# The recurrent block of a hybrid decoder trunk: one written-out order on all engines, the softplus at another place, the first transfers in another order

## Chip, cores and metric

The kernel runs on one core of a Trainium2 chip. The metric is the device time of one execution in microseconds (us), as the median of the runs. Beside it stands one profiled execution, whose trace gives the start, the duration and the releaser of instructions on each engine: TensorE (PE in the rows; PEld is its weight load), VectorE (DVE), ScalarE (ACT), GpSimd (POOL), and SyncE (SP), which issues the DMAs.

## Reference

Two layers over a sequence of 1024 positions and 1024 channels: a recurrent block (RG-LRU) with a feed-forward network, then stick-breaking attention with a feed-forward network; RMS norms lie ahead of each part. The change touches the recurrent block of the first layer:

```python
def rg_lru_block(x, w_in, b_in, conv_w, conv_b, gate_w, gate_b, lam, w_out, b_out):
    u = jnp.einsum("bsd,de->bse", x, w_in) + b_in
    gate_branch, rec = u[..., :LRU_WIDTH], u[..., LRU_WIDTH:]
    rec = causal_depthwise_conv(rec, conv_w, conv_b)             # 4 taps
    rec_blk = rec.reshape(bsz, seq, N_LRU_BLOCKS, LRU_BLOCK)     # 4 blocks of 256
    gl = jnp.einsum("bsnc,gncd->gbsnd", rec_blk, gate_w).reshape(2, bsz, seq, LRU_WIDTH)
    r_gate, i_gate = jax.nn.sigmoid(gl[0] + gate_b[0]), jax.nn.sigmoid(gl[1] + gate_b[1])
    log_a = -LRU_C * r_gate * jax.nn.softplus(-lam)
    a = jnp.exp(log_a)
    b = jnp.sqrt(-jnp.expm1(2.0 * log_a)) * (i_gate * rec)
    _, h = lax.associative_scan(_linear_recurrence_combine, (a, b), axis=1)
    y = jax.nn.gelu(gate_branch, approximate=True) * h
    return jnp.einsum("bse,ed->bsd", y, w_out) + b_out
```

## The kernel before

**Layout and products.** Everything is kept transposed, with channels on the 128 partitions and positions along the row, in halves of 512 positions (`NB`; n = 0, 1). A product of fp32 numbers is made of three matmuls in a rounded fp32 type (fp32r): high by high (L128), high weight by low data (L129), low weight by high data (L130). So each weight of 128x1024 is loaded into a raw tile by SyncE, cast on ScalarE (`whi`, L115), and its low half (`wlo`, L119) is a subtraction on VectorE. Data are split likewise: `xh`, `xl` for the normed input and later for the block's output, `rh`, `rl` for the recurrent columns. Weights stand in a ring of six tiles, that is three weights; raw tiles are three.

**Start (L249–L323).** The input and the weights of the first four columns (`FIRST`) are loaded in eight slices. As each slice k arrives, ScalarE casts (`fh`, `xh`) and squares it, VectorE makes the low halves and adds the squares into `sacc`, and TensorE adds the slice's matmuls for the four columns, first half. Then the sum of squares over channels is made by TensorE with a column of ones (`column_stats`, L192–L197, in the rows `a_ps<-ones,sacc`). VectorE works out the row factors 1/rms (`ms`, `rs_s`, `rs_t`, `rcol`, L161–L170), TensorE spreads them over the partitions (`spread`, L172, in the rows `a_ps<-ident,rcol`), and VectorE copies them from PSUM into `rbc0` and `rbc1` (L312). Both row factors borrow one bank, `bank`, which is the second half of the fourth column; the matmuls of the second halves (`second`) stand between them. Here the order on all engines is that of the code (`manual_schedule`, L249).

**Softplus (L332–L366).** Some 40 operations of VectorE on 128x8 values give the decay constants `cc` and `ch` from lambda, and the bias of the convolution `cb` and `nbias`, by a row of operations of which each needs the one before. They stand behind the start in the code, where a scheduler places every engine's instructions but TensorE's; it has put them between the rows of the start.

**The block (L326–L475).** For eight column tiles e of 128 channels there are four kinds of steps, in the order of a written string (L473): A e projects recurrent column e and makes the four convolution taps (L397–L409: VectorE's `u` halves by `rbc` L401, ScalarE's first tap, three taps on VectorE L405, then `rh` and `rl` L408); B e projects gate column e (`gb`, L447) and takes its GELU; G b makes the gates of columns 2b and 2b+1 from both (`g_ps`), and for each the values `ga`, `gt`, `gs` (L429–L439) and the scan into `y` (L440); Y e multiplies `y` by the GELU (L452). `ptile` (L383) hands out PSUM: `psA` and `psB` (`psl[0]`, `psl[1]`) hold two tiles of two banks each, and fill all eight banks; the pools take turns, two tiles each. TensorE runs in the order of the string, written by hand; where instructions of the other engines stand is the scheduler's choice.

**Last column (L455–L470).** B7 is projected half by half, each into a tile of its own from `psl[1]` (L459). Behind a half, VectorE multiplies by `rbc` (L461), ScalarE takes the GELU, and the whole output of that half is split for the next product: `xh` on ScalarE (L466), `xl` on VectorE (L467). Behind the first half the first three weights of the output projection are loaded and split (`Mix`, L140–L158).

**Output projection (L670–L701).** It closes the pools of the block, opens six tiles of one bank (`ob_ps`) in their place, and goes through 16 output tiles, each with 24 matmuls over k = 0 to 7 (`dense_in`, L132), which need `xh` and `xl` of that k; VectorE then adds bias and residual (L699). From here on the change alters nothing.

Of the kernel before, what the change touches and what calls it, by code (L numbers as in the profile page):

```python
# [31 lines left out]
FIRST = (ND, ND + 1, 0, ND + 2)  # L32


@with_exitstack
def trunk(
# [95 lines left out]
    def dense_in(ps, w, n, nk=ND):  # L132
        for k in range(nk):
            mm3(ps, w[0][:, k], w[1][:, k], xh[k][n], xl[k][n], k == 0, k == nk - 1)
# [112 lines left out]

    lc = lst.enter_context(tc.tile_pool(name="lc", bufs=1))
    with ExitStack() as st, tc.manual_schedule(engines={E.PE, E.Activation, E.DVE, E.Pool, E.SP}):  # L249
# [34 lines left out]
        for i in range(8):  # L284
# [32 lines left out]
        second(0, range(4, ND))  # L317
        column_stats(sacc[1], bank, 1)
        second(1, range(4))
        spread_to(1)  # L320
        second(1, range(4, ND))
        second(2, range(ND))
        second(3, range(ND))  # L323


    with ExitStack() as st:  # L326
        lp = st.enter_context(tc.tile_pool(name="lp", bufs=1, reuse_waits="tile"))
        sm = lambda name: lc.tile([P, ND], F32, name=name)
        V = nc.vector
# [35 lines left out]
        for j in range(3):  # L365
            V.tensor_scalar_mul(nbias[:, :, j], bin_rec, -1.0)  # L366

        col = lambda base, i: vc[:, base + i : base + i + 1]
# [4 lines left out]
        def load_gate(b):  # L373
            raw = rp.tile([P, D], F32, tag="raw", name="rawg")
            nc.sync.dma_start(raw, lru_gate_w[b])
            hi, lo = split(raw)
            v4 = lambda t: t.rearrange("p (g k c) -> p g k c", g=2, k=2)
            return v4(hi), v4(lo)


# [7 lines left out]
        def project_col(j):  # L388
            w = load_cols(lru_w_in[j])
            ps = ptile("a_ps")  # L390
            for n in range(NH):
                project(ps, w, n)
            return ps


        def stage_a(e):
            ps = pa.pop(ND + e) if ND + e in pa else project_col(ND + e)  # L397
            u = lp.tile([P, S + 16], F32, tag="u", name="u", bufs=2)
            V.tensor_copy(u[:, 0:3], nbias[:, e, 0:3])
            for n in range(NH):  # L400
                V.tensor_mul(u[:, 3 + n * NB : 3 + (n + 1) * NB], half(ps, n), rbc[n])  # L401
            rc = wide("rec", 3)
            nc.scalar.activation(rc, u[:, 3 : S + 3], AF.Identity, bias=cb[:, e : e + 1], scale=col(V_CW + 3 * ND, e))
            for j in range(3):
                V.scalar_tensor_tensor(rc, u[:, j : j + S], col(V_CW + j * ND, e), rc, op0=ALU.mult, op1=ALU.add)  # L405
            rh, rl = wide("rh", 3, F32R), wide("rl", 3, F32R)
            nc.scalar.copy(rh, rc)
            V.tensor_sub(rl, rc, f32(rh))  # L408
            rec[e], rech[e], recl[e] = rc, rh, rl  # L409


        def stage_g(b):
            gh, gl = load_gate(b)
            for i in range(2):
                e = 2 * b + i
                c = slice(i * P, (i + 1) * P)
                pss = []
                for g in range(2):
                    ps = ptile("g_ps")
# [23 lines left out]
        def stage_b(e):  # L443
            ps = pa.pop(e) if e in pa else project_col(e)
            gb = wide("gb", 3)
            for n in range(NH):
                V.tensor_mul(half(gb, n), half(ps, n), rbc[n])  # L447
# [1184 lines left out]
```

## Time and profile before

| what | value |
|---|---|
| runs | median 2216.97 us (2216.7 to 2217.77, 3 runs) |
| profiled execution | 2218.56 us |
| its span, first to last instruction | 2216.8 us |
| mean granted clock of TensorE | 0.992 |
| TensorE busy | 2177.2 us (98%), 10050 matmuls |
| VectorE busy | 1721.9 us (78%) |
| ScalarE busy | 1152.7 us (52%) |
| GpSimd busy | 224.1 us (10%) |
| DMA | 273.50 MB, mean 123 GB/s |

The stretch that the change touches is about the first 250 us of the span: the first matmul of the output projection starts at 242.78 us. In a row of the timeline the first number is the start in us from the span's beginning, the second the duration; then come engine, line of the code, operation, what is written and read, and in brackets how long the engine had been idle and what ended that. Rows that group instructions give the busy time and the mean of one in ns behind a bar, and the idle time ahead of them behind a second. A row with a window gives there the span of the window, the busy time of the instructions asked for (with their number), the granted clock, the DMA share and GB/s. Rows of waits give the total, the number and the longest.

### The profile page before, as it was taken

How to read it: one execution, taken by the hardware profiler on the slowest of the kernel's cores; microseconds unless marked ns; L12 is line 12 of the kernel's file. 1: busy time of each engine (PE TensorE's matmuls, PEld its weight loads, DVE VectorE, ACT ScalarE, POOL GpSimd, SP SyncE). 2: the span in 40 equal slices, each digit the busy share in tenths (PEclk: the TensorE clock that was granted, in tenths of full speed). 3: DMA queues.
4: the chain of work that ended last, by engine and by line, in shares of the span. 5: the costliest groups of instructions: out<-in, count | busy, mean ns of one | idle time of the engine just before them, and what ended most of it. 6: DMA issues, size and time to landing. Idle time of an engine off the chain costs nothing.

```text
span 2216.8 us, 28236 instructions
## 1 busy us (share of the span) xinstructions
PE 2177.2 (98%) x10050; PEld 1805.3 (81%) x10050; DVE 1721.9 (78%) x2412; ACT 1152.7 (52%) x2033; POOL 224.1 (10%) x356
## 2 busy tenths in 40 slices
PE   9899999999999999999999999999999999999997
PEld 7788888888888888878888888878888888888886
DVE  7877778677777887868888888866876777788886
ACT  5657545344444544646666666653534444454455
POOL 0000020000000000003333333421000000000001
PEclk9999999999999999999999999989999999999998
DMA  4021312334444864453333333631133444466442
GB/s 172 10 67 48 124 38 72 105 119 157 143 155 131 278 192 122 145 143 86 88 94 97 104 86 105 186 125 61 46 106 120 152 147 146 145 237 228 126 145 86
DMA packets 132316, 273.50 MB, mean 123 GB/s; under 512 B 15312, under 2 KB 22608, under 8 KB 132176
## 3 DMA queue, kind: packets, MB, share of 16 engines
q1 hardware_dynamic: 131600, 270.86, 38.9%
q8 instruction: 79, 1.29, 0.2%
q10 hardware_dynamic: 576, 0.85, 0.1%
q14 instruction: 61, 0.50, 0.1%
HBM read 175.70 MB, written 70.78 MB: 111 GB/s over the span
## 4 chain that ended last, share of the span: by engine, by line
PE 83%; DVE 9%; ACT 4%; DMA 2%; issue 1%; SPq 1%; DVEq 0%; ACTq 0%
PE p_ps L130 18%; PE p_ps L128 18%; PE p_ps L129 18%; PE qk_ps L130 3%; PE qk_ps L128 2%; PE qk_ps L129 2%; PE ob_ps L129 2%; PE ob_ps L128 2%; PE ob_ps L130 2%; PE wt_ps L1454 2%; PE a_ps L130 2%; PE a_ps L128 2%; PE a_ps L129 2%; DVE F L1442 2%; PE z_ps L1417 1%
## 5 line engine op out<-in xcount | busy, mean ns | idle before, releaser
L1443 POOL TENSOR_TENSOR w<-w,F 128x128 f32<-128x128 f32 (+1 forms) x192 | 184.6, 962 | 314.9 <-DVE F L1440 176.1
L128 PE MATMUL p_ps<-vh,wbh 128*128 128x512 f32 x524 | 204.3, 390 | 2.0 <-ACT ta L1003 2.0
L130 PE MATMUL p_ps<-vh,wcl 128*128 128x512 f32 x524 | 204.2, 390 | 0.5 <-DVE wcl L630 0.5
L130 PE MATMUL p_ps<-vh,wbl 128*128 128x512 f32 x524 | 204.3, 390 | 0.0
L130 PE MATMUL p_ps<-vh,wal 128*128 128x512 f32 x524 | 204.1, 390 | 0.1
L128 PE MATMUL p_ps<-vh,wch 128*128 128x512 f32 x524 | 204.1, 390 | 0.0
L128 PE MATMUL p_ps<-vh,wah 128*128 128x512 f32 x524 | 203.9, 389 | 0.0
L129 PE MATMUL p_ps<-vl,wch 128*128 128x512 f32 x524 | 203.9, 389 | 0.0
L129 PE MATMUL p_ps<-vl,wbh 128*128 128x512 f32 x524 | 203.9, 389 | 0.0
L129 PE MATMUL p_ps<-vl,wah 128*128 128x512 f32 x524 | 203.9, 389 | 0.0
L616 ACT CAST wbh<-sb 128x1024 fp32r<-128x1024 f32 (+2 forms) x69 | 69.6, 1009 | 192.6 <-DVE sb L600 192.6
L1440 DVE TENSOR_TENSOR_SCAN F<-F,unit 128x128 f32<-128x128 f32 (+3 forms) x128 | 126.9, 992 | 5.4 <-ACT F L1436 5.4
L1463 ACT CAST th<-wt_ps 128x512 fp32r<-128x512 f32 x192 | 93.3, 486 | 71.8 <-PE wt_ps L1454 69.8
L1464 DVE TENSOR_TENSOR tl<-wt_ps,th 128x512 fp32r<-128x512 f32 x192 | 105.1, 548 | 28.9 <-ACT th L1463 27.8
L128 PE MATMUL qk_ps<-vh,whi 128*128 128x512 f32 x264 | 118.8, 450 | 0.6 <-ACT vh L208 0.6
L128 PEld LDWEIGHTS p_ps<-vh,wbh 128*128 128x128 f32 x524 | 98.4, 188 | 22.6 <-ACT ta L1003 2.5
L130 PEld LDWEIGHTS p_ps<-vh,wcl 128*128 128x128 f32 x524 | 98.4, 188 | 21.8 <-DVE wcl L630 1.4
L130 PEld LDWEIGHTS p_ps<-vh,wbl 128*128 128x128 f32 x524 | 98.4, 188 | 21.7 <-DVE wbl L620 1.3
L130 PEld LDWEIGHTS p_ps<-vh,wal 128*128 128x128 f32 x524 | 98.4, 188 | 21.4 <-DVE wal L611 1.0
L129 PEld LDWEIGHTS p_ps<-vl,wah 128*128 128x128 f32 x524 | 98.4, 188 | 20.3
L129 PEld LDWEIGHTS p_ps<-vl,wch 128*128 128x128 f32 x524 | 98.4, 188 | 20.3
L128 PEld LDWEIGHTS p_ps<-vh,wah 128*128 128x128 f32 x524 | 98.4, 188 | 20.3
(408 smaller groups left out, 5725.9 us busy)
## 6 DMA issues: line engine op xcount, KB each, us to landing
raw<-in_ffn_w_in SPq DMA_DIRECT2D x88, 512.0 KB, 3.8
vl<-pd SPq DMA_DIRECT2D x128, 256.0 KB, 3.7
pd<-U SPq DMA_DIRECT2D x90, 256.0 KB, 2.3
raw<-in_ffn_w_out SPq DMA_DIRECT2D x28, 512.0 KB, 4.1
raw<-in_attn_w_qkv SPq DMA_DIRECT2D x24, 512.0 KB, 3.6
acc<-pd SPq DMA_DIRECT2D x28, 256.0 KB, 2.6
pph<-rbc SPq DMA_DIRECT2D x28, 256.0 KB, 2.5
ppl<-acc SPq DMA_DIRECT2D x28, 256.0 KB, 2.6
```

Of the source, the lines that this page charges most:

```text
L128: nc.tensor.matmul(ps, lhsT=wh, rhs=mh, start=first, stop=False, **kw)
L129: nc.tensor.matmul(ps, lhsT=wh, rhs=ml, start=False, stop=False, **kw)
L130: nc.tensor.matmul(ps, lhsT=wl, rhs=mh, start=False, stop=last, **kw)
L616: nc.scalar.copy(self.full(self.wb), self.full(self.sb))
L1417: nc.tensor.matmul(ps[:, 0 : c1 - c0], lhsT=lhsT, rhs=KL[q][hx][:, c0:c1], start=False, stop=True)
L1440: nc.vector.tensor_tensor_scan(rev, rev, unit[:, NB - n :][:, ::-1], first, op0=ALU.mult, op1=ALU.add)
L1442: nc.vector.tensor_tensor_scan(rev, rev, rev, first, op0=ALU.mult, op1=ALU.bypass)
L1443: nc.gpsimd.tensor_mul(wt, wt, F[:, 1 : n + 1])
L1454: nc.tensor.transpose(tp[:, c : c + P], W[q, hx, j, kb // 4][:, (kb % 4) * P : (kb % 4 + 1) * P], ident)
L1463: nc.scalar.copy(th[:, q0:], tp[:, q0:])
L1464: nc.vector.tensor_sub(tl[:, q0:], tp[:, q0:], f32(th)[:, q0:])
```

## The change

**The block's order.** Each operation of the block becomes a task of a list planner (`Plan`), with an engine, a duration in us, the tasks it waits for, and a rank. `emit` goes through the tasks in time: of those whose predecessors are placed it takes the one that can begin first (then the lowest rank), and emits it. The block stands under `manual_schedule` for TensorE, ScalarE, VectorE and GpSimd, so that this order is that of the program on all of them. `lru_plan` writes the tasks in the order of the same string. A DMA takes 2.6 us from issue to landing in the plan, an engine's hand-over 0.15 us, a change of ScalarE's function table 1.3 us.

```diff
+class Plan:
+    def emit(self):
+        left, end, free, table = set(range(len(self.tasks))), {}, dict(self.free), {}
+        while left:
+            best = None
+            for i in left:
+                eng, us, _, after, rank, tab = self.tasks[i]
+                if any(a not in end for a in after):
+                    continue
+                begin = max([free[eng], *(end[a] + (0.0 if self.tasks[a][0] == eng else 0.15) for a in after)])
+                if tab is not None and table.get(eng) != tab:
+                    begin += 1.3
+                key = (begin, rank, i)
+                if best is None or key < best:
+                    best = key
...
+def lru_plan(plan, order, fn):
+    col, rank = 5.44, {w: i for i, w in enumerate(order)}
...
+    def weights(i):
+        w = wants[i]
+        r = rank.get(w, len(order)) - 2.5
+        ld = plan.add("dma", 2.6, fn["load", w], [lo.get(i - 3), loads.get(i - 1)], r)
+        hi = plan.add("act", 1.05, fn["hi", w], [ld, his.get(i - 1), used.get(i - 3)], r)
+        lo[i] = plan.add("dve", 1.16, fn["lo", w], [hi], r)
...
+                rh = plan.add("act", 1.05, fn["rh", e], [t, GE.get((e - 3) // 2)], r)
+                rl[e] = plan.add("dve", 1.16, fn["rl", e], [rh], r)
...
+                    need = [pe, wt, rl[e // 2 * 2], rl[e // 2 * 2 + 1], *freed[cur % 4]]
+                    pe = plan.add("pe", col / 2, fn["pg", e, g], need, s_)
...
+    for n in range(NH):
+        pe = plan.add("pe", col, fn["pe", last, n], [pe, lo[i] if i in lo else weights(i), *freed[cur % 4]], r)
+        if n == 0:
+            used[i] = pe
+        m = plan.add("dve", 0.62, fn["bm", ND - 1, n], [pe, Y.get(ND - 4), Y.get(ND - 2)], r)
...
+            c = plan.add("act", 0.58, fn["xh", d, n], [y, pe], r)
+            plan.add("dve", 0.62, fn["xl", d, n], [c], r)
...
+    for k in range(3):
+        weights(wants.index(f"out{k}"))
```

(`used[i]` is the task behind which the tiles of weight i count as free.) The operations are those of before, as small functions; two of them, and the last column's tiles, which come from `ptile` now and so take part in the turn of the two pools:

```diff
+        def pe_last(w, n):
+            PS[w, n] = ptile("a_ps")
+            project(PS[w, n], W[w], n)
...
+        def b_half(e, n):
+            if n == 0:
+                gel[e] = wide("gb", 3)
+            w = f"B{e}"
+            ps = half(PS[w], n) if e < ND - 1 else half(PS[w, n], n)
+            V.tensor_mul(half(gel[e], n), ps, rbc[n])
...
-                ps = psl[1].tile([P, S], F32, tag="b", name="a_ps")
-                project(ps, w, n)
...
-        with tc.manual_schedule(engines={E.PE}):
+        with tc.manual_schedule(engines={E.PE, E.Activation, E.DVE, E.Pool}):
+            plan = Plan(pe=27.5, dve=37.5, act=31.0, dma=20.0)
...
+            plan.emit()
```

On VectorE, at the end of the block, the new list ends its work for the last column with these rows (`xl_0` and `xl_1` are the low halves of the output's first and second 512 positions, the names y the scan results, of which y_605 is column 7's, `gb` the GELU columns, `rbc_81` and `rbc_82` the row factors of the two halves):

```order
L640 TENSOR_TENSOR xl_1_109<-y_600,xh_1_93 128x512
L640 TENSOR_TENSOR xl_1_111<-y_601,xh_1_95 128x512
L640 TENSOR_TENSOR xl_1_113<-y_602,xh_1_97 128x512
L640 TENSOR_TENSOR xl_1_115<-y_603,xh_1_99 128x512
L637 TENSOR_TENSOR y_604<-y_604,gb 128x1024
L607 TENSOR_TENSOR gb<-a_ps,rbc_81 128x512
L632 TENSOR_TENSOR gs<-gs,gt 128x1024
L633 SCALAR_TENSOR_TENSOR y_605<-ga,gs 128x1024
L640 TENSOR_TENSOR xl_0_116<-y_604,xh_0_100 128x512
L638 TENSOR_TENSOR y_605<-y_605,gb 128x512
L607 TENSOR_TENSOR gb<-a_ps,rbc_82 128x512
```

Ahead of these rows stand eight more `xl`, and ahead of them `wlo` of the third output weight. In the list of before, from the scan of the last column on (y_603 there), the same place reads:

```order
L440 SCALAR_TENSOR_TENSOR y_603<-ga,gs 128x1024
L467 TENSOR_TENSOR xl_0_112<-y_600,xh_0_96 128x512
L452 TENSOR_TENSOR y_602<-y_602,gb 128x1024
L467 TENSOR_TENSOR xl_0_114<-y_601,xh_0_98 128x512
L465 TENSOR_TENSOR y_603<-y_603,gb 128x512
L156 TENSOR_TENSOR wlo<-raw,whi 128x1024
L467 TENSOR_TENSOR xl_0_116<-y_602,xh_0_100 128x512
L467 TENSOR_TENSOR xl_0_118<-y_603,xh_0_102 128x512
L156 TENSOR_TENSOR wlo<-raw,whi 128x1024
L461 TENSOR_TENSOR gb<-a_ps,rbc_82 128x512
L467 TENSOR_TENSOR xl_1_105<-y_596,xh_1_89 128x512
L467 TENSOR_TENSOR xl_1_107<-y_597,xh_1_91 128x512
```

The copy of the second half (`gb<-a_ps,rbc_82`) stood ahead of all `xl_1` rows, behind two of the output weights' low halves. It now stands behind the third weight's low half, twelve `xl` of both halves, column 7's scan and five rows around it, and is the nineteenth row after the weight's.

On TensorE, at the same place, the list of the change goes from the last column to the output projection like this (`a_ps_1743` is the tile of the last column's second half, `ob_ps_1910` the first output tile; the words in brackets are the engines on which a row waits):

```order
L268 MATMUL a_ps_1743<-xh7_1_103,whi_1585 128x512
L269 MATMUL a_ps_1743<-xl7_1_119,whi_1585 128x512
L270 MATMUL a_ps_1743<-xh7_1_103,wlo_1586 128x512
L268 MATMUL ob_ps_1910<-xh0_0_88,whi_1669 128x512 [waits DVE_49,Activation_49]
L269 MATMUL ob_ps_1910<-xl0_0_104,whi_1669 128x512
L270 MATMUL ob_ps_1910<-xh0_0_88,wlo_1670 128x512
```

and that of before, with `a_ps_1771` and `ob_ps_1908`, like this:

```order
L128 MATMUL a_ps_1771<-xh7_1_103,whi_1704 128x512
L129 MATMUL a_ps_1771<-xl7_1_119,whi_1704 128x512
L130 MATMUL a_ps_1771<-xh7_1_103,wlo_1706 128x512
L128 MATMUL ob_ps_1908<-xh0_0_88,whi_1759 128x512 [waits Activation_49]
L129 MATMUL ob_ps_1908<-xl0_0_104,whi_1759 128x512 [waits DVE_49]
L130 MATMUL ob_ps_1908<-xh0_0_88,wlo_1760 128x512
L128 MATMUL ob_ps_1908<-xh1_0_90,whi_1759 128x512 [waits Activation_49]
L129 MATMUL ob_ps_1908<-xl1_0_106,whi_1759 128x512 [waits DVE_49]
```

No matmul moved; the first output matmul now has a wait for VectorE beside that for ScalarE. Its tile is in both programs the first bank of the block's PSUM. The tile of the second half of B7 was one of `psB` in the program of before, and is the one of `psA` that begins at that bank in the program of the change.

**The third pair of gates.** On VectorE, ahead of the gates of columns 4 and 5, whose last low half is `rl` (`u` and `gb` read halves of A5 and B3, `rec` are taps, `gs`, `gt` and y belong to the gates of columns 2 and 3), the list of the change has, behind the first `u` half of A5 and four rows on `ga` and `gt`:

```order
L600 SCALAR_TENSOR_TENSOR gt<-ga 128x1024
L541 TENSOR_TENSOR wlo<-raw,whi 128x1024
L574 TENSOR_TENSOR u<-a_ps,rbc_82 128x512
L583 SCALAR_TENSOR_TENSOR rec<-u,vc,rec 128x1024 x2
L632 TENSOR_TENSOR gs<-gs,gt 128x1024
L633 SCALAR_TENSOR_TENSOR y_600<-ga,gs 128x1024
L632 TENSOR_TENSOR gs<-gs,gt 128x1024
L633 SCALAR_TENSOR_TENSOR y_601<-ga,gs 128x1024
L583 SCALAR_TENSOR_TENSOR rec<-u,vc,rec 128x1024
L541 TENSOR_TENSOR wlo<-raw,whi 128x1024
L607 TENSOR_TENSOR gb<-a_ps,rbc_81 128x512
L623 TENSOR_TENSOR rl<-rec,rh 128x1024
```

and that of before, from the first `u` half of A5 on to the row ahead of its `rl`, with two `u` rows of A6 among them:

```order
L401 TENSOR_TENSOR u<-a_ps,rbc_81 128x512
L439 TENSOR_TENSOR gs<-gs,gt 128x1024
L401 TENSOR_TENSOR u<-a_ps,rbc_82 128x512
L440 SCALAR_TENSOR_TENSOR y_599<-ga,gs 128x1024
L452 TENSOR_TENSOR y_598<-y_598,gb 128x1024
L405 SCALAR_TENSOR_TENSOR rec<-u,vc,rec 128x1024
L119 TENSOR_TENSOR wlo<-rawg,whi 128x1024
L405 SCALAR_TENSOR_TENSOR rec<-u,vc,rec 128x1024
L401 TENSOR_TENSOR u<-a_ps,rbc_81 128x512
L405 SCALAR_TENSOR_TENSOR rec<-u,vc,rec 128x1024
L401 TENSOR_TENSOR u<-a_ps,rbc_82 128x512
L119 TENSOR_TENSOR wlo<-raw,whi 128x1024
```

The two `u` halves of A5 stood two rows apart and its taps close behind; now six rows of the gates ahead and a weight's low half stand between the two halves, two pairs of `gs` and scan between the second tap and the third, and a `gb` half of B3 ahead of `rl`.

**Softplus.** It stands in the code between the first row factors and the second statistics (new L456 to L495), under the fixed order of the start:

```diff
         spread_to(0)
-        second(0, range(4, ND))
-        column_stats(sacc[1], bank, 1)
...
+        V.scalar_tensor_tensor(az, lam, -1.0, lam, op0=ALU.mult, op1=ALU.max)
...
+            V.tensor_scalar_mul(nbias[:, :, j], bin_rec, -1.0)
+        second(0, range(4, ND))
+        column_stats(sacc[1], bank, 1)
```

On VectorE the list of before has, from the first `ms` on (`rcol` are the row factors, `kq` a value of the softplus):

```order
L196 TENSOR_SCALAR ms<-a_ps 128x4
L350 SCALAR_TENSOR_TENSOR kq<-kq,gq 128x8 x2
L166 RECIPROCAL rs_s<-rs_s 128x4
L350 SCALAR_TENSOR_TENSOR kq<-kq,gq 128x8
L167 TENSOR_TENSOR rs_t<-rs_s 128x4
L350 SCALAR_TENSOR_TENSOR kq<-kq,gq 128x8
L168 TENSOR_TENSOR rs_t<-rs_t,ms 128x4
L350 SCALAR_TENSOR_TENSOR kq<-kq,gq 128x8
L169 TENSOR_SCALAR rs_t<-rs_t 128x4
L350 SCALAR_TENSOR_TENSOR kq<-kq,gq 128x8
L170 TENSOR_TENSOR rcol<-rs_s,rs_t 128x4
L351 SCALAR_TENSOR_TENSOR pq<-kq,pq 128x8
```

and the copy of `rbc_81` and the second `ms` follow five rows later. The list of the change has, around the second `ms`:

```order
L490 TENSOR_TENSOR cb<-cb,vc 128x8
L491 TENSOR_TENSOR cb<-cb,vc 128x8
L492 TENSOR_TENSOR cb<-cb,vc 128x8
L493 TENSOR_TENSOR cb<-cb,vc 128x8
L495 TENSOR_SCALAR nbias<-vc 128x8 x3
L336 TENSOR_SCALAR ms<-a_ps 128x4
L306 RECIPROCAL rs_s<-rs_s 128x4
L307 TENSOR_TENSOR rs_t<-rs_s 128x4
L308 TENSOR_TENSOR rs_t<-rs_t,ms 128x4
L309 TENSOR_SCALAR rs_t<-rs_t 128x4
L310 TENSOR_TENSOR rcol<-rs_s,rs_t 128x4
L453 COPY rbc_82<-a_ps 128x512
```

The rows of the softplus stood ahead of the first `ms` and between the first factors' rows; all 42 now lie between the copy of `rbc_81` and the second `ms`, these being the last.

**First transfers.** ScalarE's queue took the first slice of weights and the table of vectors; now it takes the first slice of the input, and SyncE's queue takes the table, then weights and input by turns. The cast of the first slice's weights moves to VectorE, and there are ten warm-up matmuls on `bank` for eight.

```diff
-        nc.scalar.dma_start(f4(fr[0]), lru_first[0])
-        nc.scalar.dma_start(vc, table)
+        nc.scalar.dma_start(xr[0][0], x[0, 0])
+        nc.sync.dma_start(vc, table)
         for k in range(ND):
-            nc.sync.dma_start(xr[k][0], x[k, 0])
+            nc.sync.dma_start(f4(fr[k]), lru_first[k])
             if k:
-                nc.sync.dma_start(f4(fr[k]), lru_first[k])
+                nc.sync.dma_start(xr[k][0], x[k, 0])
...
-            nc.scalar.copy(fh[k], fr[k])
+            (nc.scalar.copy if k else V.tensor_copy)(fh[k], fr[k])
```

**First output tiles.** The first four tiles of the output projection are taken together: each first gets its matmuls for k = 0 to 5, then each in turn those for k = 6 and 7.

```diff
+                            if k == 0:
+                                four = [pp.tile([P, NB], F32, tag="p", name="ob_ps") for _ in dn]
+                                for t, (d_, n_) in zip(four, dn):
+                                    dense_in(t, mix.w[d_], n_, range(ND - 2))
+                            ps = four[k]
+                            dense_in(ps, mix.w[d], n, range(ND - 2, ND))
```

More of the change, by code (lines that the diff above doesn't have):

```diff
@@ L366, in trunk @@
             V.tensor_scalar_mul(nbias[:, :, j], bin_rec, -1.0)
+        second(0, range(4, ND))
+        column_stats(sacc[1], bank, 1)
+        second(1, range(4))
+        spread_to(1)
+        second(1, range(4, ND))
+        second(2, range(ND))
+        second(3, range(ND))
+    with ExitStack() as st:
+        lp = st.enter_context(tc.tile_pool(name="lp", bufs=1, reuse_waits="tile"))
         col = lambda base, i: vc[:, base + i : base + i + 1]
```

302 lines of the change are left out of this document (209 added, 93 removed).

## Prediction

> **What bounds the kernel now.** I read the page first: shares by engine, then the chain that ended last.
>
> ```profile
> span 2216.8 us, 28236 instructions
> PE 2177.2 (98%) x10050; PEld 1805.3 (81%) x10050; DVE 1721.9 (78%) x2412; ACT 1152.7 (52%) x2033; POOL 224.1 (10%) x356
> PE 83%; DVE 9%; ACT 4%; DMA 2%; issue 1%; SPq 1%; DVEq 0%; ACTq 0%
> ```
>
> TensorE is busy for 98% of the span and makes 83% of the chain. The change adds two 128-column warm-up matmuls and takes none away, so it can only act on the 39.6 us in which TensorE stands idle (2216.8 − 2177.2) and on the clock at which it runs. The second view is TensorE's waits in the stretch that the change touches (0 to 260 us):
>
> ```profile
> PE a_ps L130 <- DVE wlo L119: 5.6, 1, 5.6
> PE a_ps L129 <- DVE xl L272: 1.6, 1, 1.6
> PE a_ps L175 <- DVE rcol L170: 1.2, 1, 1.2
> PE a_ps L128 <- ACT xh L269: 1.1, 1, 1.1
> PE ob_ps L129 <- DVE xl L467: 0.2, 1, 0.2
> ```
>
> That is all there is to win: one wait of 5.6 us for the low half of a weight, about 2.7 us at the first matmuls, 1.2 us at the first row factors. The stretch after the 5.6 us wait costs more than the wait, as busy time by window shows (the column after the count is the granted clock):
>
> ```profile
> 95.00:104.00 9.00, 9.00 (x41) 1.00 0.00 0
> 104.30:109.84 5.54, 0.00 (x0) 0.90 0.00 0
> 109.84:115.60 5.76, 5.76 (x14) 0.50 0.47 136
> 115.60:125.00 9.40, 9.40 (x43) 1.00 0.23 87
> ```
>
> For 5.76 us the clock is at half. Matmuls of 512 columns then start every 0.43 us, at full clock every 0.23 us (the starts in these timeline rows):
>
> ```profile
> 1444.59 0.63 PE L129 MATMUL ob<-vl,whi 128*128 128x512 f32 x1
> 1445.02 0.63 PE L130 MATMUL ob<-vh,wlo 128*128 128x512 f32 x1
> 242.78 0.39 PE L128 MATMUL ob_ps<-xh,whi 128*128 128x512 f32 x1
> 243.01 0.39 PE L129 MATMUL ob_ps<-xl,whi 128*128 128x512 f32 x1
> ```
>
> So 5.76 us did the work of 3.1, a loss of 2.7 us. VectorE is nearly full beside TensorE here, and its list therefore decides what comes late.
>
> **The change part by part.** The sum is made against the profiled execution (2218.56 us, span 2216.8); the median of the runs is 2216.97, and the shift is carried over to it.
>
> (a) *The wait of 5.6 us goes.* Its weight in the timeline, both halves:
>
> ```profile
> 103.69 1.05 ACT L115 CAST whi<-raw 128x1024 fp32r<-128x1024 f32 x1 [2.98 <-PE a_ps L129]
> 108.57 1.22 DVE L119 TENSOR_TENSOR wlo<-raw,whi 128x1024 fp32r<-128x1024 f32 x1
> ```
>
> ScalarE's cast was done at 104.74, and VectorE made the low half only at 108.57, behind other rows. In the new lists that half stands ahead of its column with a column's time to spare, and what stands there late instead is (d). Gain 5.6 + 2.7 = 8.3 us; bounds 5.6 and 8.4.
>
> (b) *Start, softplus.* The rows of the row factors now:
>
> ```profile
> 36.40 0.16 DVE L196 TENSOR_SCALAR ms<-a_ps 128x4 f32<-128x4 f32 x1
> 37.04 0.16 DVE L167 TENSOR_TENSOR rs_t<-rs_s 128x4 f32<-128x4 f32 x1
> 37.24 0.16 DVE L168 TENSOR_TENSOR rs_t<-rs_t,ms 128x4 f32<-128x4 f32 x1
> 37.85 1.16 PE L175 MATMUL a_ps<-ident,rcol 128*128 128x128 f32 x8 [1.16 <-DVE rcol L170]
> 41.63 0.95 PE L194 MATMUL a_ps<-ones,sacc 128*128 128x1 f32 x8
> 45.31 1.05 PE L175 MATMUL a_ps<-ident,rcol 128*128 128x128 f32 x8
> ```
>
> The softplus leaves the stretch ahead of the first factors (some 30 small rows at 0.08 to 0.2 us, and one weight half of 1.1 us less), so I put them 2.4 us earlier, at 35.4. It now stands whole between the first factors and the second `ms`: some 37 rows that each need the one before, at 0.20 us a step (37.04 to 37.24), and five at 0.08, 7.8 us. With the factor matmuls and their copy (1.2 + 0.6) ahead and 1.5 us from `ms` to `rcol` behind (36.40 to 37.85), the second factors come at 35.4 + 11.1 = 46.5, against 45.31: a loss of 1.2 us, whatever the start gains. That is the answer for the new order of the first transfers and for the ten warm-up matmuls too: matmuls that begin 1.5 to 4 us sooner meet this wait. Bounds 0 and 2.5.
>
> (c) *Clock at that wait.* From 35.4 TensorE has 1.2 us of factors, 24 matmuls at 0.23 and 0.95 of statistics, 7.6 us: it is done at 43.0 and idle for 3.5 us. No wait of that length stands in this stretch. The nearest below is 2.9 us, where the clock did fall; the nearest above is the 5.6 us wait, with its 2.7 us:
>
> ```profile
> 1440.81 1.12 PE L1389 MATMUL vt_ps<-ident,t 128*128 128x128 f32 x4 [2.91 <-DVE t L1364]
> 1436.00:1440.00 4.00, 1.90 (x10) 1.00 1.05 395
> 1440.00:1453.60 13.60, 10.16 (x34) 0.50 0.56 200
> ```
>
> I take 1.5 us, between 0 and 2.7, since the matmuls resume about when the clock falls rather than after.
> The Trainium skill, in "TensorE: Matmul & The Clock Gate" (Part 1, The HAM clock gate), has the clock fall after an idle window of about 3.4 us that runs free of the kernel. By that rule 3.5 us of idle seldom hold a whole window, and the sum below would be 1.5 us less. The trace speaks against it: the clock fell behind 2.9 us of idle.
>
> (d) *Third pair of gates.* VectorE's list takes the first half of a column's tile well ahead of the second, but in the rows of before such a reader waits for the whole tile:
>
> ```profile
> DVE gb L447 <- PE a_ps L130: 15.9, 4, 5.6
> ```
>
> 5.6 us is one more half of 24 matmuls at 0.23. If that holds for A5, VectorE stands idle until both halves are done, then has in order u, six gate rows, `wlo`, u, the wait for ScalarE's tap, two taps, two pairs of `gs` and scan, a tap, `wlo`, gb and `rl`: by the durations quoted in (e) and for a tap by this row 24.8 us in all.
>
> ```profile
> L405 DVE SCALAR_TENSOR_TENSOR rec<-u,vc,rec 128x1024 f32<-128x1024 f32 x24 | 30.5, 1282 | 0.2
> ```
>
> TensorE has two columns ahead of these gates (21.8) and 0.9 us of matmuls that need only the even tile: it waits 2.1 us. Bounds 0 (the reader gets its half at once) and 5.
>
> (e) *The end of the block*, the largest term. In the row lists of the change TensorE's first `ob_ps` matmul waits for VectorE, and of before it does not. The tile of the last column's second half used to come from the second pool; now the turn of the pools gives it the first one, where `ob_ps` starts. So `ob_ps` waits for VectorE's last copy (L607). Before, that copy ran 6 us after `ob_ps` had begun (at 242.78, in a row above), and nothing waited for it:
>
> ```profile
> 249.03 0.70 DVE L461 TENSOR_TENSOR gb<-a_ps,rbc 128x512 f32<-128x512 f32 x1
> 237.00:250.00 13.00, 12.81 (x57) 1.00 0.13 41
> ```
>
> In the new list it stands behind 19 rows, the first of which, `wlo` of the third output weight, cannot start until TensorE is done with the last column: that weight takes the last column's place in a ring of three. Durations (mean ns) from the groups of 225 to 256 us:
>
> ```profile
> L155 ACT CAST whi<-raw 128x1024 fp32r<-128x1024 f32 x3 | 3.1, 1047 | 0.5 <-PE a_ps L129 0.5
> L156 DVE TENSOR_TENSOR wlo<-raw,whi 128x1024 fp32r<-128x1024 f32 x3 | 3.7, 1226 | 0.0
> L467 DVE TENSOR_TENSOR xl<-y,xh 128x512 fp32r<-128x512 f32 x16 | 10.3, 696 | 0.7 <-ACT xh L466 0.7
> L452 DVE TENSOR_TENSOR y<-y,gb 128x1024 f32<-128x1024 f32 x1 | 1.2, 1227 | 0.0
> L461 DVE TENSOR_TENSOR gb<-a_ps,rbc 128x512 f32<-128x512 f32 x2 | 1.4, 694 | 0.0
> L439 DVE TENSOR_TENSOR gs<-gs,gt 128x1024 f32<-128x1024 f32 x2 | 2.4, 1224 | 2.0 <-ACT gt L437 2.0
> L440 DVE TENSOR_TENSOR_SCAN y<-ga,gs 128x1024 f32<-128x1024 f32 x2 | 4.6, 2292 | 0.1
> L465 DVE TENSOR_TENSOR y<-y,gb 128x512 f32<-128x512 f32 x2 | 1.4, 699 | 0.0
> 249.63 4.31 DVE L467 TENSOR_TENSOR xl<-y,xh 128x512 fp32r<-128x512 f32 x7
> ```
>
> Seven `xl` take 4.31 us, 0.60 a step (VectorE starts the next row 0.09 before the last ends). From TensorE's last matmul: cast 1.05, `wlo` 1.2, twelve `xl` 7.2, y 1.1, gb 0.6, gs 1.2, scan 2.2, `xl` 0.6, y 0.6, gb 0.7, and 0.2 of hand-overs: **15.6 us** by VectorE's rows with no wait between. Three hand-overs and one slow start of an `xl` behind ScalarE add about 0.9: 16.5 us. I take ScalarE's casts and square root to end ahead of the rows that need them. Bounds 12 (the cast finds its place before the column's last matmuls, by half of the twelve `xl`, 3.6 us) and 19 (the square root is late by the 2.0 us of L439's row, and 0.5 more).
>
> (f) *Clock after it.* 16.5 us idle is three times the 5.6 us wait, so 2.7 us are lost again; bounds 1.5 and 3.4. The 0.2 us wait of before at `ob_ps` goes, since the first four output tiles now leave the last two slices for later; from there on both programs have the same rows, TensorE-bound, and nothing takes the delay back.
>
> Sum: −8.3 + 1.2 + 1.5 + 2.1 + 16.5 + 2.7 − 0.2 = **+15.5 us**, that is 2216.97 + 15.5 = 2232.
>
> **The rivals.** *TensorE is not held at the end* (the side of the gain): the first output matmul's wait for VectorE is met early, by a row ahead of the twelve `xl`. For it speaks that the wait is printed without the row that it names; against it, that bank and order agree. Then (e) and (f) fall away: 15.5 − 19.2 = −3.7, 2213, not slower. It decides from a wait of about 4 us: the other terms are a gain of 3.7, and only a longer wait makes the kernel slower. *The clock stays up over 3.5 us of idle*: (c) is zero, 2231; for it speaks the 1.2 us wait without a fall, against it the fall behind 2.9 us. *More such waits*: the list has VectorE wait at the first half of several tiles, as the 15.9 us row has it four times already; if two more reach TensorE as in (d), with a fall of the clock at one, 2232 + 2 x 2.1 + 1.5 = 2238. Against it: most columns have a whole column's slack behind them.
>
> **How the numbers follow.** Forecast 0.50, clock up 0.30, more waits 0.13, not held 0.07. Range: the bounds of (b), (c), (d) and (f) seldom fall together; (e) alone moves it by −4.5 and +2.5, and the low end also takes in (c) at zero and some of (d): 2225; the high end is the rival with more waits: 2238. A measurement of this kernel tells about 0.2% (4.4 us) from no change: 2213 is −0.17%, so of the 0.07 most is "same": 0.05, and 0.02 faster; slower 0.93.
>
> **What would show it.** In the changed kernel's waits of TensorE a row `ob_ps` L268 from DVE gb L607 with 15 to 18 us, and half clock in the window behind it; a row for `rcol` L310 with about 3.5 us in its longest; no row of 5 us for `wlo`; a wait of about 2 us at `g_ps` for `rl`. If the first row is missing or under 4 us, (e) is wrong, and with it the sign. If the second factors come before 45.3, (b) is.

## The result, and the profile after

The changed kernel takes 2230.82 us (median of 4 runs, 2227.97 to 2233.80) against 2217.37 us for the kernel before in the same set (4 runs): a ratio of 1.0060, 95% interval 1.0043 to 1.0078. It is slower by 13.5 us. The profiled execution, the slowest of the four, took 2233.80 us, with a span of 2232.0 us against 2216.8.

The page of the changed kernel shows TensorE with nearly the same busy time as before (2176.1 us; before 2177.2) in a longer span:

```profile
span 2232.0 us, 28249 instructions
PE 2176.1 (97%) x10054; PEld 1803.0 (81%) x10054; DVE 1727.5 (77%) x2413; ACT 1149.8 (52%) x2030; POOL 225.4 (10%) x356
```

The difference is idle time of TensorE. Its waits in the first 260 us (total, number, longest):

```profile
PE ob_ps L268 <- ACT xh L639: 16.6, 1, 16.6
PE a_ps L315 <- DVE rcol L310: 5.4, 2, 3.3
PE a_ps L426 <- POOL ident masks.py:199: 1.4, 1, 1.4
PE g_ps L269 <- DVE rl L623: 1.3, 1, 1.3
PE g_ps L268 <- ACT rh L589: 0.5, 1, 0.5
PE a_ps L269 <- DVE xl L413: 0.2, 1, 0.2
```

The row of 5.6 us for `wlo` is gone, `rcol` has grown from 1.2 to 5.4 us in two waits, `g_ps` has two rows that were not there, and the first `ob_ps` waits for 16.6 us. A lower clock stands behind three of these places, as the busy time by window shows (the column after the count is the granted clock):

```profile
44.00:48.00 4.00, 2.57 (x13) 0.86 0.00 0
48.00:52.00 4.00, 4.00 (x14) 0.72 0.24 65
160.00:164.00 4.00, 2.24 (x8) 0.86 0.40 121
164.00:168.00 4.00, 4.00 (x14) 0.71 0.03 10
256.00:260.00 4.00, 3.30 (x8) 0.50 0.99 340
260.00:264.00 4.00, 4.00 (x16) 0.76 0.84 321
```

Where the time went is read best from the starts of the same matmuls in the timelines of the two profiled executions (`e8_all` is an experiment below):

| first matmul of | before | change | difference | e8_all |
|---|---|---|---|---|
| first row factors (`rcol`) | 37.85 | 34.53 | −3.3 | 32.58 |
| second row factors | 45.31 | 45.43 | +0.1 | 41.27 |
| first pair of gates | 71.03 | 72.81 | +1.8 | 67.00 |
| second pair of gates | 123.11 | 116.33 | −6.8 | 110.52 |
| column behind the third pair | 177.50 | 174.63 | −2.9 | 164.91 |
| output projection (`ob_ps`) | 242.78 | 256.70 | +13.9 | 230.19 |
| feed-forward (`p_ps`) | 330.31 | 346.27 | +16.0 | 317.23 |
| end of the span | 2216.8 | 2232.0 | +15.2 | 2202.0 |

The change was 6.8 us ahead at the second gates. It lost 3.9 us at the third pair, 16.8 at the end of the block and 2.0 behind it.

The long wait is best seen from VectorE's timeline, as the prediction had listed its rows:

```profile
240.96 1.23 DVE L541 TENSOR_TENSOR wlo<-raw,whi 128x1024 fp32r<-128x1024 f32 x1 [1.08 <-ACT whi L537]
242.10 7.48 DVE L640 TENSOR_TENSOR xl<-y,xh 128x512 fp32r<-128x512 f32 x12
249.49 1.22 DVE L637 TENSOR_TENSOR y<-y,gb 128x1024 f32<-128x1024 f32 x1
250.63 0.68 DVE L607 TENSOR_TENSOR gb<-a_ps,rbc 128x512 f32<-128x512 f32 x1
251.23 1.22 DVE L632 TENSOR_TENSOR gs<-gs,gt 128x1024 f32<-128x1024 f32 x1
252.48 2.29 DVE L633 TENSOR_TENSOR_SCAN y<-ga,gs 128x1024 f32<-128x1024 f32 x1
255.88 0.68 DVE L607 TENSOR_TENSOR gb<-a_ps,rbc 128x512 f32<-128x512 f32 x1
```

On ScalarE and TensorE at the same place:

```profile
255.99 0.62 ACT L639 CAST xh<-y 128x512 fp32r<-128x512 f32 x1 [2.07 <-DVE y L638]
256.70 0.77 PE L268 MATMUL ob_ps<-xh,whi 128*128 128x512 f32 x1 [16.63 <-ACT xh L639]
```

VectorE's copy of the last column's second half ends at 256.56, ScalarE's cast of column 7 at 256.61, TensorE starts at 256.70. The profile names the cast, which came last; the prediction had named the copy. Two candidates 0.05 us apart can't be told apart by looking; the next two experiments separate them.

### The profile page after: what moved, and what is told of

It is laid out like the page before. It is cut to its first block, busy times and chain, and to the rows that moved or that the text cites. A ratio compares the mean times of both kernels' runs of the same rounds, so it can differ in the third digit from the quotient of the medians.

```text
span 2232.0 us, 28249 instructions
## 1 busy us (share of the span) xinstructions
PE 2176.1 (97%) x10054; PEld 1803.0 (81%) x10054; DVE 1727.5 (77%) x2413; ACT 1149.8 (52%) x2030; POOL 225.4 (10%) x356
## 4 chain that ended last, share of the span: by engine, by line
PE 83%; DVE 10%; ACT 3%; issue 2%; DMA 1%; SPq 1%; DVEq 0%; ACTq 0%
PE p_ps L270 18%; PE p_ps L268 18%; PE p_ps L269 18%; PE ob_ps L268 2%; PE ob_ps L269 2%; PE ob_ps L270 2%; PE qk_ps L270 2%; PE qk_ps L268 2%; PE qk_ps L269 2%; PE wt_ps L1641 2%; DVE F L1629 2%; PE a_ps L268 2%; PE a_ps L270 2%; PE a_ps L269 2%; PE z_ps L1604 1%
## 5 line engine op out<-in xcount | busy, mean ns | idle before, releaser
L1651 DVE TENSOR_TENSOR tl<-wt_ps,th 128x512 fp32r<-128x512 f32 x192 | 105.0, 548 | 26.2 <-ACT th L1650 24.8
L269 PEld LDWEIGHTS p_ps<-vl,wbh 128*128 128x128 f32 x524 | 98.5, 188 | 20.5
```

The lines of the kernel that those rows point to most:

```text
L269: nc.tensor.matmul(ps, lhsT=wh, rhs=ml, start=False, stop=False, **kw)
L1651: nc.vector.tensor_sub(tl[:, q0:], tp[:, q0:], f32(th)[:, q0:])
```

## The experiments

Each time is a median of its runs; the ratio is against the kernel before on the same chip (medians there 2215.98 to 2216.30 us).

### Which instruction holds the output projection: e1_pool, e2_copy

`e1_pool` undoes only the pool turn:

```diff
         def pe_last(w, n):
-            PS[w, n] = ptile("a_ps")
+            PS[w, n] = psl[1].tile([P, S], F32, tag="b", name="a_ps")
```

> Only the pool turn of the last column is undone: both halves of B7 come from psB again; the lists stay. Theory (the first output tile takes the bank that VectorE's last copy still reads): the 16.6 us wait at the first ob_ps goes. What is left there by the lists: xl of the first column ends at 242.8, TensorE is done at 240.1, so about 2.7 us; and the second output tile, which takes a bank of the first half's tile, meets the copy of the first half, which ends at 251.3: about 4.4 us more. Together 7 us for 16.6, 2221 us, and 2218 to 2219 if the clock stays up at such short waits. Rival (the wait is for ScalarE's xh of column 7, as the profile's row names it): no row of ScalarE or VectorE moves, so the wait stays at 16 to 17 us and the time at 2231.

Measured: 2220.88 us, ratio 1.0020 (1.0011 to 1.0029). Its waits of TensorE from 225 us on:

```profile
PE ob_ps L268 <- DVE gb L607: 4.3, 1, 4.3
PE ob_ps L268 <- ACT xh L639: 1.4, 1, 1.4
PE ob_ps L269 <- DVE xl L640: 0.8, 1, 0.8
PE a_ps L268 <- DVE gb L607: 0.5, 1, 0.5
```

Its first output matmul and its cast of column 7 in the timelines:

```profile
240.81 0.51 PE L268 MATMUL ob_ps<-xh,whi 128*128 128x512 f32 x1 [1.43 <-ACT xh L639]
```

```profile
255.31 0.62 ACT L639 CAST xh<-y 128x512 fp32r<-128x512 f32 x1 [2.07 <-DVE y L638]
```

No row of ScalarE or VectorE changed its place, and the 16.6 us are gone: TensorE starts 14.5 us ahead of the cast of column 7. What is left is 2.2 us for the first `xh` and `xl`, 4.3 us at the second tile, which meets the copy of the first half, and 0.5 us inside the last column, whose second half now waits for an earlier `gb` copy. The rival falls.

`e2_copy` leaves the pools and moves the copy in the list:

```diff
-        m = plan.add("dve", 0.62, fn["bm", ND - 1, n], [pe, Y.get(ND - 4), Y.get(ND - 2)], r)
+        m = plan.add("dve", 0.62, fn["bm", ND - 1, n], [pe, Y.get(ND - 4)], r)
```

> Only the list: the two copies of the last column no longer wait for the product of column 6, so that the copy of the second half stands behind seven short rows instead of nineteen; the pools stay as in the change. Theory (TensorE waits for that copy): 242.1 + 0.6 (first half) + 3.6 (six xl) + 0.7 = 247.0, a wait of 7 us for 16.6, and by 9.6 us less 2221 us; the clock falls as before. Rival (ScalarE's xh of column 7): column 7's product still stands behind twelve xl, the scan and column 6, so the wait stays at 15 to 17 us and the time within 2 us of 2231.

Measured: 2220.66 us, ratio 1.0022 (1.0013 to 1.0031). VectorE's copy, ScalarE's first cast of column 7 and TensorE's start in its timelines:

```profile
244.48 0.68 DVE L607 TENSOR_TENSOR gb<-a_ps,rbc 128x512 f32<-128x512 f32 x1
```

```profile
254.65 0.62 ACT L639 CAST xh<-y 128x512 fp32r<-128x512 f32 x1 [3.56 <-DVE y L638]
```

```profile
245.31 0.76 PE L268 MATMUL ob_ps<-xh,whi 128*128 128x512 f32 x1 [7.17 <-ACT xh L639]
```

The wait ends 0.15 us behind the copy, as its new place gives, and 9.3 us ahead of the cast of column 7. The row still names ScalarE, by some other cast of the same line: where several semaphores are waited for, the name is that of the last event ahead of the start. TensorE waited for the bank that VectorE had yet to read.

### The softplus: e4_soft

```diff
         spread_to(0)
-        V.scalar_tensor_tensor(az, lam, -1.0, lam, op0=ALU.mult, op1=ALU.max)
...
-            V.tensor_scalar_mul(nbias[:, :, j], bin_rec, -1.0)
         second(0, range(4, ND))
         column_stats(sacc[1], bank, 1)
         second(1, range(4))
         spread_to(1)
+        V.scalar_tensor_tensor(az, lam, -1.0, lam, op0=ALU.mult, op1=ALU.max)
...
+            V.tensor_scalar_mul(nbias[:, :, j], bin_rec, -1.0)
```

> The change with the softplus moved behind the second row factors; all else as in the change. Theory (the softplus holds the second factors back): the 3.3 us wait at the second rcol goes, and with it the lower clock of 0.86 and 0.72 between 44 and 52 us, worth 1.7 us; the softplus' 7.8 us find cover in the 6.9 us in which VectorE waits at 56.6 for B0. 5 us less: 2226. Rival (the 7.8 us only move on, and the first gates come late by them): the wait at rcol goes, one of 3 to 7 us appears at the first g_ps, and the time stays within 2 us of 2231.

Measured: 2225.87 us, ratio 1.0041 (1.0028 to 1.0053): 5 us less than the change. The two intervals overlap, so the trace decides: its first gates start at 67.4 us for 72.8. Its waits at the row factors and the gates, and its clock where the change's had fallen:

```profile
PE a_ps L315 <- DVE rcol L310: 1.9, 1, 1.9
PE g_ps L269 <- DVE rl L623: 1.3, 1, 1.3
PE g_ps L268 <- ACT rh L589: 0.5, 1, 0.5
```

```profile
44.00:48.00 4.00, 4.00 (x19) 1.00 0.02 4
48.00:52.00 4.00, 4.00 (x19) 1.00 0.00 0
```

The 3.3 us wait and the lower clock are gone and nothing new came at the gates: the softplus costs nothing where VectorE waits for B0.

### The third pair of gates: e6_gates

```diff
-                m = [plan.add("dve", 0.62, fn["um", e, n], [c, parts[n]], r) for n in range(NH)]
+                m = [plan.add("dve", 0.62, fn["um", e, n], [c, parts[-1]], r) for n in range(NH)]
...
-                m = [plan.add("dve", 0.62, fn["bm", e, n], [parts[n], Y.get(e - 3), B.get(e - 1)], r - 1) for n in range(NH)]
+                m = [plan.add("dve", 0.62, fn["bm", e, n], [parts[-1], Y.get(e - 3), B.get(e - 1)], r - 1) for n in range(NH)]
```

> The planner is told that a reader of a column's first half waits for both halves; all else as in the change. Theory (the third gates come late since VectorE's list has it stand idle for half a column ahead of A5): the waits of 1.3 and 0.5 us at g_ps go, the 16.6 us wait at ob_ps stays within 0.5 us, and the time falls by 1.8 us, to 2229; by 3 if the clock falls less often at about 160 us. Rival (another list, another late row): a new wait of 1 us or more among the gates, 2230 to 2232.

Measured: 2227.83 us, ratio 1.0052 (1.0040 to 1.0065), 3 us below the change, though the two intervals overlap; the trace decides. Its waits, all of them:

```profile
PE ob_ps L268 <- DVE gb L607: 16.5, 1, 16.5
PE a_ps L315 <- DVE rcol L310: 4.5, 2, 2.5
PE a_ps L426 <- POOL ident masks.py:199: 1.4, 1, 1.4
```

Both rows at `g_ps` are gone, and no other came. Here the row at `ob_ps` names VectorE's copy, with the same 16.5 us. From the second gates to the column behind the third this kernel takes 54.40 us (115.88 to 170.28), as before (54.39); the change took 58.30.

### The start: e7_start, f3_oldtransfers

`e7_start` is the kernel before with the transfers, warm-up matmuls and softplus as the diff of the change shows them.

> The kernel before with the start of the change (first transfers, warm-up matmuls, place of the softplus), its block still placed by the scheduler. Theory (the start costs up to 2 us and gains nothing, the list gains the 5.6 us wait, the pool turn costs 16.6): the second rcol comes at 45 to 46 us, the wait of 5 to 6 us for wlo stays with its half clock, there is no wait over 1 us at ob_ps, and the time is 0 to 2 us above before: 2216.5 to 2218.5. Rival (the start takes part in the gain at the gates): the wait for wlo goes, 2208 to 2210.

Measured: 2217.74 us, ratio 1.0009 (1.0000 to 1.0018).

```profile
PE a_ps L130 <- DVE wlo L119: 5.5, 1, 5.5
PE a_ps L175 <- DVE rcol L170: 5.5, 2, 3.8
```

The second factors came at 46.93 us, a little later than expected; the wait for `wlo` stayed, and there was none over 0.2 us at `ob_ps`. So the gain of the change between the first and second gates is the list's, and the loss at the end is not the start's.

`f3_oldtransfers` is `e8_all` (below) with the old transfers, the old cast of the first slice and eight warm-up matmuls:

```diff
-        nc.scalar.dma_start(xr[0][0], x[0, 0])
-        nc.sync.dma_start(vc, table)
+        nc.scalar.dma_start(f4(fr[0]), lru_first[0])
+        nc.scalar.dma_start(vc, table)
...
-        for i in range(10):
+        for i in range(8):
```

> e8_all with the first transfers, the cast of the first slice and the eight warm-up matmuls as before the change. Theory (the new order gains at the start, and the change loses it again at the second factors): the first statistics come at 32 to 33 us for 28.9, nothing behind takes it back, and the time is 3.5 to 4.5 us above e8_all, 2207.5. Rival (the gain came from the softplus leaving that stretch): within 1 us of e8_all, 2204.

Measured: 2206.23 us, ratio 0.9950 (0.9937 to 0.9962), 2.5 us above `e8_all`. Its first statistics start at 30.78 us, against 28.89 in `e8_all` and 32.85 before: the transfers are worth 1.9 us there, less than expected. The other 2 us go with the softplus, which left that stretch: before, its rows stand ahead of VectorE's first `xl`, which starts at 7.77 us for 6.32 here. Both theories had a share. Neither share is VectorE's or the queues' alone, though: TensorE's 512-column matmuls start every 0.43 us until 13.0 us before and until 10.3 in `f3_oldtransfers`, and every 0.23 us from there; in `e8_all` they start every 0.23 us from about 7 us on. So a part of each share is the length of this slow stretch, and no run separates it.

### All of it mended: e8_all

On top of the edits of `e1_pool`, `e2_copy`, `e4_soft` and `e6_gates`:

```diff
-        if n == 0:
-            used[i] = pe
+        used[i] = pe
...
-        if n == 0:
-            used[i] = pe
     for k in range(3):
...
+        column_stats(sacc[0], bank, 0)
         for k in range(ND):
             x_square(k, 1)
             x_add(k, 1)
...
-        column_stats(sacc[0], bank, 0)
```

> The change with every late row mended: last column from psB, softplus behind the second factors, the first statistics ahead of the second half's sums on VectorE, and a planner that knows three things (the last weight's tiles come free after both halves, a reader of a first half waits for both, the last column's copy does not wait for column 6). Theory: of the change's waits in the first 260 us (2.1 + 3.3 at rcol, 1.8 at the gates, 16.6 at ob_ps) some 1 us is left, at the second statistics; with the lower clock behind them (2.7 and 1.7) that is 2230.8 - 27 = 2204, 12 us below before. Rival (the delays only hide one another): new waits of 4 us and more in the block, 2210 or above.

Measured: 2203.74 us (2203.09 to 2205.03), ratio 0.9946 (0.9934 to 0.9959): 12.2 us below before. Its waits in the first 262 us, and its first page lines:

```profile
PE a_ps L423 <- POOL ident masks.py:199: 1.4, 1, 1.4
PE a_ps L331 <- DVE rbc L451: 1.1, 1, 1.1
```

```profile
span 2202.0 us, 28243 instructions
PE 2169.6 (99%) x10054; PEld 1799.6 (82%) x10054; DVE 1727.9 (78%) x2413; ACT 1147.9 (52%) x2029; POOL 225.1 (10%) x356
```

### The end alone, and the clock behind it: f1_tail, e3_fill, e5_fill2, f2_tail_fill

`f1_tail` is `e8_all` with the change's pool turn and its rules for the last column.

> e8_all with the end of the block as in the change again (last column's tiles by the turn of the pools, the planner's two rules for the last column as in the change). Theory (the end alone costs the wait and the clock behind it): one wait of 16.5 us at ob_ps, 2.7 us of half clock behind it, no other new wait: 2203.7 + 16.5 + 2.7 = 2223. Rival (much of the wait is taken back later): under 2216.

Measured: 2221.79 us, ratio 1.0026 (1.0017 to 1.0035): 18 us above `e8_all` for one wait of 16.5 us, named here as the copy:

```profile
PE ob_ps L268 <- DVE gb L607: 16.5, 1, 16.5
```

Three kernels fill the wait with matmuls that nothing reads:

```diff
             plan.emit()
+            junk = psl[1].tile([P, S], F32, tag="b", name="junk")
+            for i in range(50):
+                nc.tensor.matmul(junk[:, 0:P], lhsT=ident, rhs=ident, start=True, stop=True)
```

> The change with 50 idle matmuls (128 columns, fp32, into a bank of psB that nothing reads) behind the last column on TensorE: at 0.29 us each they fill 14.5 of the 16.6 us and hold nothing up. Theory (the half clock behind the wait comes from the idle time): the first ob_ps comes at the same 256.7 us, the clock stays at 1.00 behind it, and the time falls by 2.7 us to 2228. Rival (the matmuls are slow there since DMA is at a share of 1.05 in the same stretch): the slow stretch stays, 2231.

Measured: 2232.21 us, ratio 1.0068 (1.0054 to 1.0082). This one could not decide: the 50 matmuls took 11.3 us, and not 14.5, so that 5.5 us stayed idle, and half clock followed. The next expectation reads 10.2 us from this run; 11.3 us is 0.226 us for each matmul, which is what 74 of them then needed.

> As e3_fill, with 74 idle matmuls for 50: they ran at 0.204 us each there (50 in 10.2 us), so 74 fill 15.1 us. Theory (the half clock comes from idle time alone): the first ob_ps still comes after 16 to 17 us from the last column's end, the clock is 1.00 behind it, and the time is 2.7 us below the change's: 2227 to 2228.5. Rival (contention with the DMA, whose share is 0.9 to 1.05 there): half clock or slow matmuls stay, 2230 to 2231.

Measured: 2230.19 us, ratio 1.0066 (1.0052 to 1.0080). The 74 matmuls took 16.7 us. By the time alone the rival's number came. The profile says otherwise: no wait is left at `ob_ps`, and the clock is full with the DMA as busy as in the change:

```profile
252.00:256.00 4.00, 3.89 (x24) 1.00 1.02 338
256.00:260.00 4.00, 4.00 (x19) 1.00 1.03 378
```

> f1_tail with 70 idle matmuls that nothing reads (0.225 us each, 15.8 us) in the wait. Nothing else in the first 260 us lowers the clock in these two. Theory (idle time lowers the clock): the first ob_ps starts as late as in f1_tail within 0.5 us, the clock stays at 1.00, and the time is 2.7 us less: 2220. Rival (DMA contention): the same as f1_tail within 0.5 us.

Measured: 2221.46 us, ratio 1.0020 (1.0011 to 1.0029). Its first `ob_ps` starts at 247.90 us and `p_ps` at 335.06, 87.2 us between them; in `f1_tail` it is 89.5 (246.34 to 335.80). With the new order of the first output tiles it is 87.0 to 87.2 us where TensorE did not wait long at `ob_ps` (`e8_all`, `f3_oldtransfers` and the two that fill the wait), and 88.6 to 89.7 where it did (the change in both profiles, `e2_copy`, `e3_fill`, `e4_soft`, `e6_gates`, `f1_tail`; `e1_pool` waits inside the stretch and is left out). In `f1_tail` the half clock stood while the DMA moved nothing (its share and GB/s are the last two columns):

```profile
244.00:248.00 4.00, 1.66 (x4) 0.50 0.00 0
248.00:252.00 4.00, 4.00 (x12) 0.60 0.58 170
```

So in the traces idle time, not the DMA, brings the half clock, and it costs 1.4 to 2.7 us. The medians do not show it: `f2_tail_fill` is 0.3 us below `f1_tail`, with intervals that overlap, as the rival said, and `e5_fill2` is not below the change. The unchanged rest of the kernel, from the first `p_ps` to the end, took between 1881.9 us (`f2_tail_fill`) and 1887.2 us (`e7_start`) in the profiled executions; an effect of 2 us is well within that scatter. How the clock ran at `ob_ps` in the runs without a profile is not known.

### The change once more: f4_change

> The change itself once more, on the same chip as these runs: 2229 to 2232, and 26 to 28 us above e8_all; the profiled execution may or may not show the lower clock at 44 us and at 160 us, since the waits there are about as long as those behind which the clock fell in some executions and not in others.

Measured: 2230.73 us, ratio 1.0060 (1.0047 to 1.0072). Its windows at the second factors and at the gates:

```profile
44.00:48.00 4.00, 2.67 (x10) 0.50 0.00 0
48.00:52.00 4.00, 4.00 (x13) 0.64 0.23 23
160.00:164.00 4.00, 2.24 (x9) 1.00 0.18 35
164.00:168.00 4.00, 4.00 (x18) 1.00 0.24 96
```

The same program as in the result's profile, with the same waits: this time the clock fell at the factors and not at the gates.

## Why the prediction was right

It forecast 2232 us (2225 to 2238) and slower; it came to 2230.8. The forecast was one mechanism with most of the sum, and that mechanism was shown. That the sums agree so closely is partly luck: two smaller terms, (b) and (d), were off by 1 to 2 us and nearly cancelled, the size of (e) holds a slip of addition, and the profiled execution with its 15.2 us is the slowest of four, while the medians lie 13.5 us apart.

| term | forecast | in the profiles |
|---|---|---|
| (a) wait for `wlo` and its clock | −8.3 | −8.6 (first to second gates: 52.08 before, 43.52 now) |
| (b) second factors later | +1.2 | +0.1 |
| (c) clock at that wait | +1.5 | +1.7 (first gates +1.8, less (b)) |
| (d) third pair of gates | +2.1 | +1.8 waits, +2.1 clock |
| (e) first `ob_ps` waits | +16.5 | +16.8, of it 16.6 in the row |
| (f) clock after it, less the old 0.2 us wait | +2.5 | +2.0 |
| rest to the end | 0 | −0.8 |
| sum | +15.5 | +15.2 of span |

- (a) was right in place and size, and `e7_start` shows that it is the list that brings it: with the scheduler's block the wait stays.
- (b) was mis-sized by 1.1 us. The step "I put them 2.4 us earlier, at 35.4" failed: the first factors came 3.3 us earlier, at 34.53, although TensorE waited 2.1 us for them. The length of the softplus was right (36.34 to 43.98, 7.6 us for 7.8 forecast), and with it that the second factors come no sooner than before, whatever the start gains: 4.3 us gained by the first statistics (32.85 to 28.60) are gone at the second.
- (c) A fall of the clock there is a matter of the execution. Six profiled executions have a wait of 3.2 to 3.3 us at the second factors. The clock fell in four of them: in both profiles of the change, with 0.72 and 0.64 in the second window, in `e1_pool` and in `e2_copy`. It stayed up in `e5_fill2` and in this one, `e3_fill`, which is the same program up to the end of the last column:

```profile
44.00:48.00 4.00, 2.77 (x16) 1.00 0.00 0
48.00:52.00 4.00, 4.00 (x19) 1.00 0.25 79
```

  That the same program differs so agrees with the Trainium skill, in "TensorE: Matmul & The Clock Gate" (Part 1, The HAM clock gate), where the clock is set by windows which run free of the kernel, so that runs differ. The rival "the clock stays up" was thus no other case but a part of the executions, two of these six.
- (d) The mechanism was right, shown by `e6_gates`, and the waits were 1.8 us for 2.1. VectorE stood idle for 5.0 us ahead of A5's first `u` half, waiting for TensorE, and took 24.6 us from there to the end of `rl` (138.29 to 162.91), for 24.8 forecast. The fall of the clock behind the waits in the result's profile, 2.1 us, was in the forecast only as a rival's part; `f4_change` does not have it, and takes 56.78 us from the second gates to the column behind the third for 58.30.
- (e) was right in mechanism, and its size in part by luck. The listed terms add up to 16.65 us, not 15.6: ScalarE's cast of 1.05 us is in the list and not in the sum. With the 0.9 us for hand-overs and a slow `xl` they would have made 17.5. The rows above run in the listed order and take 16.5 us from TensorE's end (240.07) to the copy's end (256.56), so that the terms themselves held and no further 0.9 us shows. That TensorE waits for the copy was argued from the row lists; `e1_pool` (bank moved, no row moved) and `e2_copy` (row moved, no bank moved) show it. The cause is two-fold: the bank, and a list in which the copy stands behind work that itself waits for the last column's end.
- (f) is 1.4 to 2.7 us in the traces with the wait, and not to be seen in the medians.

The rival "more such waits" did not come: TensorE's waits above hold none in the block beside (d). The rival "TensorE is not held at the end" put the kernel at 2213 without (e) and (f). `e1_pool`, without the pool turn, came to 2220.9, since 7.0 us of other waits in the same list then show (0.5, 1.4, 0.8 and 4.3); the change's own gain is to be had with the mended list of `e8_all`.

## What to carry to other kernels

When an order is written out, ask of every tile that changes its place who reads the old holder last, and where that reader stands in its engine's list: a copy that nobody waited for held the whole of TensorE, since its bank was handed on. A planner is as good as its rules: three that differed from the program (when a ring's place comes free, what a reader of half a tile waits for, one needless predecessor), together with the bank and the places of the softplus and the first statistics, stood between a gain of 12 us and a loss of 14. The rule on the ring and the place of the first statistics were changed only together with the rest, so their own shares are not known. And a gain at the start is worth only what the next wait on the same chain leaves of it.

## What the runs showed of the hardware that was not expected

- The clock fell behind much shorter idle time than the 2.9 us of the prediction. In `f2_tail_fill` it did so at the second statistics, behind a wait of 1.1 us, and in `f1_tail`, with the same wait at the same place, it did not, and the first `ob_ps` of `f1_tail` came 1.6 us sooner. The windows of `f2_tail_fill`:

```profile
36.00:40.00 4.00, 2.97 (x16) 0.91 0.00 0
40.00:44.00 4.00, 4.00 (x18) 0.67 0.00 0
```

- The idle matmuls (fp32, 128 columns) took 0.225 us each in a row (74 in 16.7 us). The 0.29 of the first expectation was worked out from the four matmuls that spread a row factor, 1.16 us together, and the 0.204 of the next from a time of 10.2 us that the trace does not show.
- Executions of one program spread over up to 8 us (2218.9 to 2227.1 in 11 runs of `e2_copy`), and `e8_all`, which has fewer waits, over 2 us in 5.
- At the start the granted-clock column does not show the slow stretch: in the kernel before it reads 1.00 from 9 to 13 us, where 512-column matmuls start every 0.43 us, as they do at 0.50 elsewhere.
